# Seven block products in place of eight: the down-projections of a two-layer encoder

## The chip, the cores and the metric

The kernel runs on one core of one Trainium2 chip. The metric is the time of one execution in device microseconds (us). Five engines work side by side, each taking its own instructions in order: TensorE (PE, matmuls and weight loads), VectorE (DVE), ScalarE (ACT), GpSimd (POOL) and SyncE (SP, which issues the large transfers).

## The reference, cut to what matters

256 positions of width 2048 pass through two layers. Each has a token mixer (layer 0: grouped-query attention, layer 1: dilated window attention) and a gated MLP; every sub-layer is preceded by an RMS norm and added to the residual `h`, and a last norm follows.

```python
def conv_ffn(h, w_up, conv_w, conv_b, w_down):
    u = h @ w_up                       # 2048 -> 2 x 5632
    u = depthwise_conv3(u, conv_w) + conv_b
    gate, val = jnp.split(u, 2, axis=-1)
    return (jax.nn.silu(gate) * val) @ w_down   # 5632 -> 2048
```

All of it is float32. The change concerns the last product, `@ w_down`, in both layers.

## The kernel before, in words

**Precision.** Each operand of a large matmul is split into a high part of type F32R and the remainder, and each product is made of three: high x high, high x low, low x high (lines 115 to 117). The activations are the stationary operand, 128 tokens at a time; a weight tile is the moving operand with 512 columns.

**A feed** (`feed`, lines 97 to 135) is the unit of work. It takes 512 rows of a weight matrix (a chunk, `kg`) by 512 columns (a block, `n`): two transfers of 512 KB into `raw` buffers (line 105), of which there are four; for each, ACT makes the high part `wh` (line 127) and DVE the remainder `wl` (line 128), in four buffers each; then 2 x 2 x 2 x 3 matmuls into two PSUM banks, one per half of the tokens. A feed has 24 matmuls, 12 for each pair of `wh` and `wl`. The splits stand in `tc.high_priority(offset=AHEAD)`, so that the framework, which fixes each engine's order when the program is built, places them ahead of other work. `project` runs the feeds of a block one after another; `project2` interleaves two blocks such that the last chunk of both comes at the end; `project_last` handles the very last block so that its output can leave in pieces.

**The MLP** (`ffn`, lines 362 to 566) runs in two halves of 6 and 5 chunks of the hidden dimension (`HALVES`). For each chunk two up-projection blocks are computed (gate and value). What follows each block is written as generators (`gate_gen`, `value_gen`, `act_split`, `flush`), which `step()` advances a piece at a time between matmul groups: evacuation by ACT (line 359), 32x32 transposes by DVE and 16 copies by POOL (`turned`, lines 401 to 408), convolution taps on ACT and DVE (lines 388 and 396), the product of gate and value on POOL (line 422), and the split of the result (lines 441 and 442), which makes the stationary operands of the down-projection. A half then ends with four down-projection blocks of 512 columns over its 6 or 5 chunks (lines 557 to 564): `project2` for blocks 0 and 1, `project` for 2 and 3, in layer 1's second half `project_last` for block 3. `done` adds a block's two banks to `h` on DVE (line 331, or 487 at the end); in the second half of layer 0 it also starts the transposition of `h` for the next mixer (`late_transpose`, lines 273 to 307: transposes at line 268, splits at 213 and 216, copies at 263 and 297). In layer 1's second half POOL multiplies the finished blocks by the final gain (line 489).

PSUM has eight banks here: four `acc` tiles and four `ps` tiles. `bias_lines` (line 866) prepares the bias table of mixer B on the side.

Of the kernel before, what the change touches and what calls it, by code (L numbers as in the profile page):

```python
# [7 lines left out]
F32 = mybir.dt.float32  # L8
# [22 lines left out]
def tile_encoder(ctx: ExitStack, tc: tile.TileContext, x, xT, w_a, w_ao, q_gain, k_gain, w_b, w_bo,  # L31
# [17 lines left out]
    ones = cpool.tile([P, P], F32, name="ones")  # L49
    nc.gpsimd.memset(ones, 1.0)  # L50
# [46 lines left out]
    def feed(accs, lhs, kg, wap, first, last, by_m=False, pieces=1, mid=None):  # L97
# [11 lines left out]
        def mms(order):  # L109
            for m, kt in order:  # L110
                (wh, wl), j = hls[kt // 2], kt % 2
                xh, xl = lhs[4 * kg + kt][:2]
                st, sp = first and kt == 0, last and kt == 3
# [159 lines left out]
    def late_transpose(hT, n, g, pool, tag):  # L273
# [5 lines left out]
        if n < 3:  # L279
            t = pool.tile([P, 4, NT], F32, tag=tag, name=nm("tT"))  # L280
# [81 lines left out]
    def ffn(l, hT, ss_in, cw, g_next, last, side=None):  # L362
        with tc.tile_pool(name=nm("fpool"), bufs=1) as fp:
            junk = junk_of(fp)
            next_space[0] = fp, ("quad", 2), ("tT", 1)
# [5 lines left out]
            if last:  # L371
                fin = fp.tile([P, D], F32, name="fin")
                nc.gpsimd.dma_start(fin, final_norm.partition_broadcast(P))
# [27 lines left out]
            def turned(s, u):  # L401
# [3 lines left out]
                for q, c in QC:  # L405
                    nc.gpsimd.tensor_copy(u[32 * c:32 * c + 32, :, :, 32 * q:32 * q + 32],  # L406
                                          quad[32 * q:32 * q + 32, c].rearrange("p (j m) t -> p j m t", m=2))
# [16 lines left out]
            def value_gen(accs, blk, gate, last):  # L424
                s = evac_scaled(fp, accs, rstd, 1)
                yield
                turned(s, blk[1])
# [8 lines left out]
            def act_split(value):  # L436
                slots, k0 = value[5:]
                cv = value[2]
                for j in range(4):
# [3 lines left out]
                    if j == 1:  # L443
                        yield

# [11 lines left out]
            kgs = list(range(4))  # L457
            for hf, (p0, p1) in enumerate(HALVES):
                slots = {}
                last_value = None  # L460
                for p in range(p0, p1):
# [16 lines left out]
                    if p == 1 and side is not None:  # L478
                        spare.append(side())
                start(flush(last_value))  # L480

                def done(accs, n):
                    if hf == 1 and last:
                        for m in range(2):
# [4 lines left out]
                            nc.gpsimd.tensor_tensor(hs, hs, fin[:, cols], ALU.mult)  # L489
# [5 lines left out]
                    if hf == 1:  # L495
                        sumsq_cols(ss, n, junk)
                        start(late_transpose(hTn, n, g_next, fp, "tT"))
# [14 lines left out]
                def put(m, c0, c1, how, r):  # L512
                    hs = h[:, m, c0:c1]
                    if how == "fin":
                        nc.vector.scalar_tensor_tensor(hs, hs, r, fin[:, c0:c1], ALU.mult, ALU.mult)
# [19 lines left out]
                def last_out(acc, parts):  # L535
# [8 lines left out]
                    nc.gpsimd.tensor_tensor(ha, ha, fin[:, 1536:1536 + NT], ALU.mult)  # L544
# [628 lines left out]
```

## Time and profile before

| | |
|---|---|
| median of 3 timed runs | 2253.71 us (2253.49 to 2254.2) |
| profiled execution, first to last instruction | 2253.4 us |
| granted TensorE clock, mean | 0.999 |
| down-projection stages, layer 0 | 519 to 650 us and 867 to 977 us |
| down-projection stages, layer 1 | 1789 to 1919 us and 2136 to 2245 us |
| moved by DMA | 439.56 MB, 195 GB/s |

The profile is one execution, whose span is given from its first to its last instruction; no other time of it is recorded. Its page lists busy time by engine, the chain of work that ended last, and the costliest groups of instructions. The trace behind it answers questions about a stretch of time (windows), about the order of instructions (timeline) and about one line. A group's row reads: line, engine, operation, output and inputs with their shapes, count, then busy us and mean ns of one, then the idle time of that engine in front of them and what ended it. A row of one line reads: count, shortest, median and longest duration in ns.

### The profile page before, as it was taken

To read this page: it belongs to the slowest core of one execution; us is meant where nothing else is said; L and a number is where in the kernel's file an instruction comes from. 1 tells how busy PE (TensorE), PEld (TensorE's weight loads), DVE (VectorE), ACT (ScalarE), POOL (GpSimd) and SP (SyncE) were. 2 spreads that over 40 slices of the span, in tenths; PEclk is the share of its full clock that TensorE was granted. 3 is DMA by queue.
4 is the path that set the end of the run, shared out by engine and by line. 5 is a ranking of instruction groups with operands and counts; after the bars stand their busy time and mean duration, and the time that the engine had idled before them with its cause. 6 is when DMAs were issued, how large, how long until landed. Compare 5 with 4: busy or idle time off the path is not lost.

```text
span 2253.4 us, 28552 instructions
## 1 busy us (share of the span) xinstructions
PE 2240.8 (99%) x10089; PEld 1860.1 (83%) x10089; DVE 1605.8 (71%) x2137; ACT 1216.2 (54%) x1691; POOL 760.4 (34%) x999
## 2 busy tenths in 40 slices
PE   9999999999999999999999999999999999999998
PEld 7888888888888888888888888888888888888887
DVE  6877967776546777878876877676777764576765
ACT  7676556555345655555454554445655543465653
POOL 2342165663006554010052007002665600256530
PEclk9999999999999999999999999999999999999999
DMA  8565665655555565565566555566555555555554
GB/s 302 191 222 172 203 201 190 195 193 195 194 193 192 194 193 188 191 215 195 184 191 195 180 187 175 180 201 211 195 193 193 193 196 192 193 195 194 191 196 150
DMA packets 125871, 439.56 MB, mean 195 GB/s; under 512 B 14232, under 2 KB 18072, under 8 KB 125600
## 3 DMA queue, kind: packets, MB, share of 16 engines
q1 hardware_dynamic: 123056, 429.05, 57.0%
q0 software_dynamic: 2384, 8.39, 1.5%
q8 instruction: 79, 1.29, 0.2%
q14 instruction: 64, 0.52, 0.1%
q10 hardware_dynamic: 288, 0.30, 0.0%
HBM read 432.34 MB, written 5.34 MB: 194 GB/s over the span
## 4 chain that ended last, share of the span: by engine, by line
PE 96%; DVE 2%; DMA 1%; issue 1%; POOL 1%; ACT 0%; SPq 0%; DVEq 0%; POOLq 0%; ACTq 0%
PE acc L116 31%; PE acc L115 31%; PE acc L117 31%; DVE wl L128 1%; DMA raw<-in_w_b_dram 1%; DVE tT L268 1%; PE ps L225 0%; PE ps L224 0%; PE ps L223 0%; PE ps L1031 0%; PE ps L221 0%; DMA raw<-in_w_a_dram 0%; ACT wh L127 0%; POOL wide L263 0%; POOL t L704 0%
## 5 line engine op out<-in xcount | busy, mean ns | idle before, releaser
L128 DVE TENSOR_TENSOR wl<-raw,wh 128x1024 fp32r<-128x1024 f32 (+1 forms) x804 | 1010.0, 1260 | 521.2 <-ACT wh L127 518.1
L127 ACT ACTIVATE wh<-raw 128x1024 fp32r<-128x1024 f32 (+1 forms) x804 | 840.8, 1050 | 800.7 <-PE acc L117 714.8
L115 PE MATMUL acc<-wh,xh 128*128 128x512 f32 x2176 | 848.7, 390 | 0.7 <-ACT wh L127 0.7
L116 PE MATMUL acc<-wl,xh 128*128 128x512 f32 x2176 | 847.6, 390 | 0.3 <-DVE wl L128 0.2
L117 PE MATMUL acc<-wh,xh 128*128 128x512 f32 x2176 | 847.3, 389 | 0.0
L406 POOL COPY u<-quad 32x256 f32<-32x256 f32 x704 | 489.4, 695 | 539.9 <-DVE quad L259 512.1
L117 PEld LDWEIGHTS acc<-wh,xh 128*128 128x128 f32 x2176 | 408.6, 188 | 85.5
L115 PEld LDWEIGHTS acc<-wh,xh 128*128 128x128 f32 x2176 | 408.8, 188 | 84.8 <-ACT wh L127 1.1
L116 PEld LDWEIGHTS acc<-wl,xh 128*128 128x128 f32 x2176 | 408.8, 188 | 84.5 <-DVE wl L128 1.4
L115 PE MATMUL acc<-wh,a 128*128 128x512 f32 x1008 | 392.8, 390 | 0.0
L116 PE MATMUL acc<-wl,a 128*128 128x512 f32 x1008 | 392.3, 389 | 0.0
L117 PE MATMUL acc<-wh,a 128*128 128x512 f32 x1008 | 392.2, 389 | 0.0
L117 PEld LDWEIGHTS acc<-wh,a 128*128 128x128 f32 x1008 | 189.2, 188 | 39.5 <-DVE a L210 0.2
L116 PEld LDWEIGHTS acc<-wl,a 128*128 128x128 f32 x1008 | 189.3, 188 | 39.0
L115 PEld LDWEIGHTS acc<-wh,a 128*128 128x128 f32 x1008 | 189.3, 188 | 38.6
L263 POOL COPY wide<-quad 32x256 f32<-32x256 f32 x165 | 107.2, 650 | 170.1 <-DVE quad L259 162.9
L422 POOL TENSOR_TENSOR cv<-cg,cv 128x1024 f32<-128x1024 f32 x22 | 71.1, 3232 | 135.7 <-DVE cv L396 135.7
L359 ACT ACTIVATE stg<-acc,rstd 128x512 f32<-128x512 f32 x122 | 82.9, 685 | 31.7 <-PE acc L117 31.7
L396 DVE SCALAR_TENSOR_TENSOR cg<-u,cw,cg 128x256 f32<-128x256 f32 x176 | 82.3, 511 | 4.5 <-ACT cg L388 4.5
L396 DVE SCALAR_TENSOR_TENSOR cv<-u,cw,cv 128x256 f32<-128x256 f32 x176 | 74.3, 479 | 15.5 <-ACT cv L388 15.3
L259 DVE STREAM_TRANSPOSE quad<-stg 128x512 f32<-128x512 f32 x88 | 59.4, 699 | 10.3 <-ACT stg L359 10.3
L268 DVE STREAM_TRANSPOSE tT<-h 32x256 f32<-32x256 f32 x144 | 62.8, 436 | 2.7
(172 smaller groups left out, 1037.0 us busy)
## 6 DMA issues: line engine op xcount, KB each, us to landing
raw<-in_w_up_dram SPq DMA_DIRECT2D x352, 512.0 KB, 4.5
raw<-in_w_down_dram SPq DMA_DIRECT2D x176, 512.0 KB, 4.2
raw<-in_w_b_dram SPq DMA_DIRECT2D x144, 512.0 KB, 4.4
raw<-in_w_bo_dram SPq DMA_DIRECT2D x48, 512.0 KB, 3.7
raw<-in_w_a_dram SPq DMA_DIRECT2D x40, 512.0 KB, 4.7
raw<-in_w_ao_dram SPq DMA_DIRECT2D x32, 512.0 KB, 4.0
raw<-in_w_a_dram SPq DMA_DIRECT2D x16, 256.0 KB, 5.8
there<-quad POOLq DMA_DIRECT2D x6, 512.0 KB, 3.2
```

Of the source, the lines that this page charges most:

```text
L115: nc.tensor.matmul(accs[m], xh[:, c], wh[:, j, :], start=st, stop=False)
L116: nc.tensor.matmul(accs[m], xh[:, c], wl[:, j, :], start=False, stop=False)
L117: nc.tensor.matmul(accs[m], xl[:, c], wh[:, j, :], start=False, stop=sp)
L127: nc.scalar.activation(wh[:, c], r[:, c], AF.Copy)
L128: nc.vector.tensor_tensor(wl[:, c], r[:, c], wh[:, c].bitcast(F32), ALU.subtract)
L259: nc.vector.transpose(quad[:, :, at, :], src.rearrange("p (x c t) -> p c x t", c=4, t=32))
L263: nc.gpsimd.tensor_copy(o[32 * c:32 * c + 32, :, 32 * q:32 * q + 32], quad[32 * q:32 * q + 32, c])
L268: nc.vector.transpose(o[cols].rearrange("p a (m t) -> p a m t", m=2)[:, :, :, rows], s[rows].rearrange("p m (a c) -> p a m c", c=P)[:, :, ...
L359: nc.scalar.activation(o[:, m, :], accs[m], AF.Copy, scale=rstd[:, m:m + 1])
L396: nc.vector.scalar_tensor_tensor(cj, halves(flat[:, j, o:o + NT])[:, ::-1], tap(n, j, i), cj, ALU.mult, ALU.add)
L406: nc.gpsimd.tensor_copy(u[32 * c:32 * c + 32, :, :, 32 * q:32 * q + 32], quad[32 * q:32 * q + 32, c].rearrange("p (j m) t -> p j m t", m=2))
L422: made.append(nc.gpsimd.tensor_tensor(cv, cg, cv, ALU.mult).ins)
```

## The change

In each half of each MLP, two of the chunks (the first and the third, `fast = (0, 2)`) are multiplied for two column blocks at a time in seven products of half-size blocks, in Winograd's form of Strassen's scheme. The 512 rows of the chunk are cut into two halves of 256, the tokens into two halves of 128, and the two column blocks are the third pair. Eight products of such blocks would be 48 matmuls; the seven are 42.

- `combined` (called by `act_split`) builds the sums of activations for the two chunks: four subtractions on DVE and three larger splits.
- `fast_unit` loads the four weight quarters of the two blocks, forms four sums of 128x1024 (two on POOL, two on DVE, one of these in place), splits seven tiles, and issues 7 x 6 matmuls into the banks of products 1 to 7.
- `fold` adds products 1, 5, 6 and 7 into `h`: one copy on ACT, four additions on DVE that read PSUM, four on POOL. Products 2, 3 and 4 share the banks into which the ordinary feeds of the remaining chunks accumulate.
- `pair` runs two blocks over all chunks in a given order and takes all eight PSUM banks. The orders differ by half; in layer 1's second half the last two blocks run both fast units first, then `project` and `project_last` over the other chunks.
- Room is made: the final gain is loaded in four pieces just before layer 1's last down-projections, into buffers of `hT`; an unused constant goes; some temporaries share buffers; nine of the sixteen copies of the last value block of each half go from POOL to ACT.

```diff
+                if k0 // 4 in fast:
+                    slots[-1 - k0 // 4] = combined(cv, k0)
+                    ready.add(k0 // 4)
...
+            def combined(cv, k0):
+                v = cv.rearrange("p (b j) (m t) -> p b j m t", b=2, m=2)
+                st = fp.tile([P, 4, 2, P], F32, tag="sum", name=nm("st"), bufs=3)
+                a11, a21, a12, a22 = v[:, 0, :, 0], v[:, 0, :, 1], v[:, 1, :, 0], v[:, 1, :, 1]
+                for o, x, y in ((0, a21, a22), (2, a21, a11), (1, a11, st[:, 0]), (3, a12, st[:, 1])):
+                    nc.vector.tensor_tensor(st[:, o], x, y, ALU.subtract)
...
+                split_in_order(*own, st)
+                split_in_order(hA, lA, v[:, :, :, 0])
+                split_in_order(hB, lB, a22)
...
+            def fast_unit(acc, pick, wap0, wap1, begun, first, end):
...
+                b11, b12, b22, b21 = load(wap0, 0), load(wap1, 0), load(wap1, 1), load(wap0, 1)
+                with tc.high_priority(offset=2 * AHEAD):
+                    t1 = new_sum()
+                    nc.gpsimd.tensor_tensor(t1, b11, b12, ALU.add)
+                    nc.vector.tensor_tensor(b12, b12, b22, ALU.add)
+                    t2 = new_sum()
+                    nc.vector.tensor_tensor(t2, b11, b12, ALU.add)
+                    t4 = new_sum()
+                    nc.gpsimd.tensor_tensor(t4, t2, b21, ALU.add)
+                for i, (q, r) in enumerate(((1, b11), (2, b21), (5, t1), (3, b22), (7, b12), (6, t2), (4, t4))):
...
+                    with tc.high_priority(offset=AHEAD):
+                        nc.scalar.activation(wh, r, AF.Copy)
+                        nc.vector.tensor_tensor(wl, r, wh.bitcast(F32), ALU.subtract)
+                    xh, xl = pick[q]
+                    for j in range(2):
...
+                        nc.tensor.matmul(acc[q], xh[:, j], wh[:, j], start=st, stop=False)
+                        nc.tensor.matmul(acc[q], xh[:, j], wl[:, j], start=False, stop=False)
+                        nc.tensor.matmul(acc[q], xl[:, j], wh[:, j], start=False, stop=sp)
+                    begun.add(q)
+                    step(i % 2 == 0)
+
+            def fold(acc, n0, n1):
...
+                nc.scalar.activation(a, acc[1], AF.Copy)
+                tt(v, acc[6], a, ALU.subtract)
+                pool(hs(0, n0), hs(0, n0), a, ALU.add)
+                tt(w, acc[7], v, ALU.add)
+                tt(c, acc[5], v, ALU.add)
+                pool(hs(0, n1), hs(0, n1), c, ALU.add)
+                tt(v, acc[5], w, ALU.add)
+                pool(hs(1, n0), hs(1, n0), w, ALU.subtract)
+                pool(hs(1, n1), hs(1, n1), v, ALU.add)
...
-                done(project2(wd, 0, 1, slots, list(range(np_)), 1, lambda a: done(a, 0)), 1)
-                for n in (2, 3):
-                    if last and hf == 1 and n == 3:
-                        project_last(wd, n, slots, list(range(np_)), first_out, last_out)
+                for n0, n1 in ((0, 1), (2, 3)):
+                    if last and hf == 1 and n0 == 2:
...
+                        for kg in fast:
+                            fast_unit(acc, slots[-1 - kg], wd[n0, kg], wd[n1, kg], begun, kg == fast[0],
+                                      range(1, 8) if kg == fast[-1] else ())
+                        fold(acc, n0, n1)
...
+                        rest = [kg for kg in range(np_) if kg not in fast]
+                        done(project(wd, n0, slots, rest), n0)
+                        project_last(wd, n1, slots, rest, first_out, last_out)
                     else:
-                        done(project(wd, n, slots, list(range(np_))), n)
+                        rest = [kg for kg in range(np_) if kg not in fast]
+                        both = {kg: [(kg, 0), (kg, 1)] for kg in rest}
+                        f0, f1 = ([(kg, None)] for kg in fast)
+                        if n0 == 0:
+                            order = both[1] + f0 + both[3] + (both[4] if np_ > 5 else []) + f1 + both[np_ - 1]
+                        elif hf == 0:
+                            order = f0 + both[1] + f1 + both[3] + both[4] + both[5]
+                        else:
+                            order = [(1, 0)] + f0 + [(3, 0)] + f1 + [(4, 0), (1, 1), (3, 1), (4, 1)]
+                        pair(wd, (n0, n1), slots, order, done)
```

More of the change, by code (lines that the diff above doesn't have):

```diff
@@ L95, in drain, with feed @@
                 step()
-    def feed(accs, lhs, kg, wap, first, last, by_m=False, pieces=1, mid=None):
+    def feed(accs, lhs, kg, wap, first, last, by_m=False, pieces=1, mid=None, begun=()):
         raws, w = [], 2048 // pieces
@@ L112, in mms @@
                 xh, xl = lhs[4 * kg + kt][:2]
-                st, sp = first and kt == 0, last and kt == 3
+                st, sp = first and kt == 0 and m not in begun, last and kt == 3
                 c = slice(m * P, (m + 1) * P)
@@ L364, in ffn @@
             junk = junk_of(fp)
[L365 removed]
+            next_space[0] = fp, ("quad", 2), ("cv", 1)
             drain(1)
```

143 lines of the change are left out of this document (104 added, 39 removed).

## The prediction

> **What bounds the kernel now.** I read the page first: busy times, then the chain, then the costliest groups.
>
> ```profile
> PE 2240.8 (99%) x10089; PEld 1860.1 (83%) x10089; DVE 1605.8 (71%) x2137; ACT 1216.2 (54%) x1691; POOL 760.4 (34%) x999
> PE 96%; DVE 2%; DMA 1%; issue 1%; POOL 1%; ACT 0%; SPq 0%; DVEq 0%; POOLq 0%; ACTq 0%
> L127 ACT ACTIVATE wh<-raw 128x1024 fp32r<-128x1024 f32 (+1 forms) x804 | 840.8, 1050 | 800.7 <-PE acc L117 714.8
> L422 POOL TENSOR_TENSOR cv<-cg,cv 128x1024 f32<-128x1024 f32 x22 | 71.1, 3232 | 135.7 <-DVE cv L396 135.7
> ```
>
> TensorE (PE) is busy throughout and is 96% of the chain. ScalarE (ACT) waits 714.8 us before L127 for PE to give back a `wh` buffer: the splits run as far ahead as four buffers let them. So fewer matmuls shorten the kernel, as long as the other engines deliver. Whether they do is read from the stages that change, the eight pairs of down-projection blocks. The windows view has one row for each: layer 0 first half, layer 0 second half, then layer 1. The last row is an up-projection.
>
> ```profile
> core 0: us, PE busy (x) PEld busy (x) DVE busy (x) ACT busy (x) POOL busy (x), PEclk, DMA share, GB/s
> 519.40:584.40 65.00, 65.00 (x289) 53.83 (x288) 42.34 (x49) 31.11 (x39) 13.93 (x17) 1.00 0.57 195
> 584.40:649.70 65.30, 65.30 (x290) 54.09 (x289) 31.84 (x29) 25.47 (x24) 0.00 (x0) 1.00 0.56 193
> 867.00:922.00 55.00, 55.00 (x244) 45.58 (x243) 39.94 (x51) 28.77 (x39) 13.92 (x17) 1.00 0.59 194
> 922.30:976.60 54.30, 54.30 (x241) 45.00 (x240) 49.60 (x80) 28.15 (x41) 0.00 (x0) 1.00 0.55 188
> 1789.00:1854.00 65.00, 65.00 (x288) 53.85 (x287) 42.34 (x48) 30.78 (x38) 13.93 (x17) 1.00 0.57 195
> 1854.00:1919.00 65.00, 65.00 (x289) 53.83 (x288) 31.54 (x29) 25.46 (x24) 0.00 (x0) 1.00 0.57 193
> 2136.00:2190.00 54.00, 54.00 (x240) 44.70 (x240) 37.29 (x45) 29.05 (x40) 16.29 (x19) 1.00 0.59 194
> 2190.00:2244.00 54.00, 54.00 (x245) 44.93 (x243) 30.70 (x30) 22.20 (x27) 7.37 (x6) 1.00 0.44 143
> 246.00:519.00 273.00, 272.96 (x1204) 225.35 (x1203) 199.03 (x254) 158.87 (x207) 149.02 (x200) 1.00 0.61 198
> ```
>
> PE never stops, at the full clock (1.00). VectorE (DVE) is second: it leaves 23 and 33 us idle in the two pairs of a six-chunk half, but only 15 and 4.7 us in layer 0's five-chunk half (rows 3 and 4).
>
> The timeline shows one period of the feeding pipeline:
>
> ```profile
> 620.13 1.06 ACT L127 ACTIVATE wh<-raw 128x1024 fp32r<-128x1024 f32 x1 [1.66 <-PE acc L117]
> 621.22 1.23 DVE L128 TENSOR_TENSOR wl<-raw,wh 128x1024 fp32r<-128x1024 f32 x1 [1.50 <-ACT wh L127]
> 622.85 1.06 ACT L127 ACTIVATE wh<-raw 128x1024 fp32r<-128x1024 f32 x1 [1.66 <-PE acc L117]
> ```
>
> The period is 2.72 us for 12 matmuls, so **0.2267 us a matmul**. A buffer is refilled 2.3 us after PE frees it (620.13 to 622.45) and needed after three further buffers, 8.2 us: the **lead is 5.8 us**.
>
> **What the change removes.** A pair's two blocks at one chunk take 48 matmuls; the seven products take 7 x 2 x 3 = 42. There are 2 fast chunks x 2 pairs x 2 halves x 2 layers = 16 units, so 96 matmuls go: 96 x 0.2267 = **21.8 us**, 2.72 per pair. The tail after the last matmul stays. The Trainium skill (TensorE: Matmul & The Clock Gate, Part 1) gives 215.7 ns from start to start for such a matmul; by it the gain would be 20.7 us. The trace has 227, and the trace decides.
>
> **What it adds on DVE and POOL.** A unit splits seven tiles instead of four and adds two sums on DVE: five more 128x1024 instructions with two SBUF inputs. It also puts two 128x1024 sums on GpSimd (POOL). Each pair gets a fold: four DVE instructions that read PSUM, and four 128x512 additions on POOL. Their prices, from the timeline of DVE and of POOL and the row of L772:
>
> ```profile
> L331 DVE TENSOR_TENSOR h<-acc,h 128x512 f32<-128x512 f32 x5 | 3.2, 681 | 0.0
> 967.99 3.49 DVE L128 TENSOR_TENSOR wl<-raw,wh 128x1024 fp32r<-128x1024 f32 x3
> 976.43 1.28 DVE L331 TENSOR_TENSOR h<-acc,h 128x512 f32<-128x512 f32 x2
> 538.04 4.55 DVE L128 TENSOR_TENSOR wl<-raw,wh 128x1024 fp32r<-128x1024 f32 x2
> 538.30 3.22 POOL L422 TENSOR_TENSOR cv<-cg,cv 128x1024 f32<-128x1024 f32 x1 [5.81 <-DVE cv L396]
> 2187.64 2.97 POOL L489 TENSOR_TENSOR h<-h,fin 128x512 f32<-128x512 f32 x2 [28.68 <-ACT junk L488]
> 2189.70 1.99 DVE L128 TENSOR_TENSOR wl<-raw,wh 128x1024 fp32r<-128x1024 f32 x1 [1.49 <-ACT wh L127]
> 409.33 3.23 POOL L422 TENSOR_TENSOR cv<-cg,cv 128x1024 f32<-128x1024 f32 x1 [6.44 <-DVE cv L396]
> 410.73 1.39 DVE L259 STREAM_TRANSPOSE quad<-stg 128x512 f32<-128x512 f32 x2 [0.44 <-ACT stg L359]
> L772 POOL TENSOR_TENSOR pr<-pr,l x14: 1032/1042/1940, 90.8 to 183.4; 128x512 f32<-128x512 f32 x14
> ```
>
> Three splits in a row take 3.49: the last shows its full 1.23, so one more occupies (3.49 - 1.23) / 2 = **1.13 us**. Two residual additions take 1.28, with one at 0.68 (row of L331): 0.60 for one more. At 538 two splits, worth 2.36, take 4.55, while L422 runs on POOL: DVE stood **2.19 us** for one POOL addition of the size that each unit gets twice. It happens again at 2189.70 with a 128x512 one. A POOL addition of 128x512 takes 1.04 undisturbed, which I take as its hold. Two transposes inside L422's next run (410.73) take 1.39, an ordinary pace: they are not held. An addition that reads PSUM, with one operand in SBUF, I count as not held either.
>
> The Trainium skill (SBUF — State Buffer, "Who interferes with whom") has the rule: a DVE instruction with two SBUF inputs and a GpSimd instruction that reads SBUF exclude each other, and the later one waits for the whole of the other. The trace agrees (4.55 for 2.36). By the Trainium skill, a DVE instruction with one SBUF input is free of it, and here too the trace agrees (the transposes at 410.73).
>
> So on DVE a unit occupies 9 x 1.13 + 2 x 2.19 = **14.6 us, against 9.5 us of PE** (42 x 0.2267). Per pair: 10 x 1.13 + 4 x 0.60 = 13.7 us of DVE work, and 4 x 2.19 + 4 x 1.04 = 12.9 us of holds.
>
> - Six-chunk halves: PE 288 x 0.2267 - 2.7 = 62.6 each. First pair 42.3 + 13.7 = 56.0, with holds 68.9; second 45.5, with holds 58.4. Sum 127.3 against 125.2.
> - Layer 0's five-chunk half: PE 240 x 0.2267 - 2.7 = 51.7 each. First pair 53.6, with holds 66.5; second 63.3, with holds 76.2. Sum 142.7 against 103.4: **39 us too much**, 13.5 of it without any hold.
> - Layer 1's: 51.0 and 44.4, with holds 63.9 and 57.3. Sum 121.2 against 103.4: **18 us too much**.
>
> **What is forgiven.** The lead of 5.8 us once per half. Holds that fall on instructions with one SBUF input: those that read PSUM, and transposes. Layer 0's second half has many transposes:
>
> ```profile
> L268 DVE STREAM_TRANSPOSE tT<-h 32x256 f32<-32x256 f32 x42 | 18.3, 436 | 0.8
> L216 DVE SCALAR_TENSOR_TENSOR xh<-tT,gain,xh 128x256 fp32r<-128x256 f32 x12 | 5.1, 478 | 0.6 <-ACT xh L213 0.6
> 542.52 0.75 DVE L442 TENSOR_TENSOR a<-cv,a 128x256 fp32r<-128x256 f32 x2
> L297 ACT ACTIVATE wide<-quad x18: 412/414/417, 264.3 to 1533.8; 32x256 f32<-32x256 f32 x18
> raw<-in_w_down_dram SPq DMA_DIRECT2D x176, 512.0 KB, 4.2
> ```
>
> With 18.3 us of transposes beside 26 us of holds I let half (13) overlap; some 5 us of transposes and their splits can slide into mixer B. Stalls of PE: layer 0 second half 39 - 13 - 5.8 - 5 = 15 (bounds 3 without holds' cost, 28 without overlap). Layer 1 second half: 18 - 5.8 - 3 (PSUM readers) = 9, and 6 more because its last pair runs both units back to back: 29.2 us of DVE against 19.0 of PE, the slack coming too late. That is 15 (bounds 3 and 24). A six-chunk half: the excess of its first pair, 68.9 - 62.6 = 6.3, is just what the lead and the PSUM readers cover; I take 1.5 each for the units that start a pair (bounds 0 and 6.3). Sum 15 + 15 + 3 = **33 us of stalls**, between 6 and 65.
>
> Edits at nothing: `combined` replaces four splits of 128x256 by four subtractions and three larger splits, some 2 us more DVE per fast chunk (four subtractions at 0.38, half of the row of L442, and an estimated 0.6 for 1792 columns of splits in place of 1024), in up-projections where DVE idles 74 of 273 us (last row of windows). Nine of the last value block's copies go from POOL to ACT, 9 x 0.41 = 3.7 us (row of L297), where ACT idles 24 to 34 us in these pairs; the lead covers them, and without it they cost that much once per half. The smaller loads of `fin`, the shared buffers and `bias_lines` stand off every path that PE waits on. The transfers are the same 2 MB per chunk; a unit holds all four `raw` buffers until its sums are done, which is priced under the second rival. A pair now holds all eight PSUM banks; the next pair's third product starts 2 x 1.36 us or more after its first, and the two residual additions in front of it (1.28) fit unless DVE is already behind, which is counted.
>
> Sum: the profiled execution's 2253.4 us of span lies 0.3 below the median of the timed runs, 2253.7; so 2253.7 - 21.8 + 33 = **2265 us**, slower by 0.5%.
>
> **Rivals.** *Holds cost nothing (faster).* POOL's sums fall into time in which DVE waits anyway, or under transposes and PSUM readers. For it: DVE alone exceeds PE only in layer 0's second half, 116.9 against 103.4; minus lead and slide (10.8) 3 us of stalls remain, and 3 for the back-to-back units: 2253.7 - 21.8 + 6 = 2238. It decides from where the holds that cost fall below 21.8 - 6 = 16 us of the 103 added. Against it: row 4 has 4.7 us of idle DVE for 13 of holds. When the sums are issued early enough the six-chunk halves give their full 10.9 in either case.
>
> *DVE's excess is paid in each unit (much slower).* A unit holds the four `raw` buffers until its sums and splits are done; if DVE is late, the next feed's loads start late, and each needs 4.2 us to land (row above), 1.06 and 1.23 for its split, 6.5 in all of the unit's 9.5. Then no lead builds up again between units: 16 x (14.6 - 9.5) = 82 us, 2253.7 - 21.8 + 82 = 2314. For it: the last unit of each layer's second half has one feed or none in front of it. Against it: the other fourteen follow two feeds or more, and two feeds with a unit are 4 x 1.13 + 14.6 = 19.1 us of DVE in 20.4 of PE. Half of that price is 2273, inside the forecast.
>
> *It takes out no matmuls* is excluded by the loop counts.
>
> **Numbers.** Forecast 0.52 (its own range 2251 to 2281: stalls midway between 33 and each bound), first rival 0.36 (2232 to 2249), second rival 0.12 (2281 to 2314). From 2237 to 2292 about 0.10 is left out below and 0.08 above. This kernel's measurement tells about 0.2% (4.5 us) from no change: below 2249.2 lies the first rival, 0.36; between, 0.10; above 2258.2, 0.54.
>
> **What would show it.** Right: 96 fewer matmuls; PE busy falling below its windows' length in the second halves, with waits of PE for `wl`; DVE over 95% there; splits of 3 us and more beside POOL's additions in the units; the six-chunk halves some 8 to 11 us shorter than now over both layers. Wrong: PE still full in all eight windows (then the first rival, 2238), or PE waiting for `raw` transfers in the six-chunk halves too (then the second). If the splits beside POOL's sums stay at 1.23 us, the step on holds has failed.

## The result, and the profile after

The changed kernel takes **2321.18 us** (median of 4 runs, 2319.83 to 2322.79) against 2253.95 (2253.49 to 2255.61) beside it: a ratio of 1.0295 (95% interval 1.028 to 1.0309), slower by 67 us. The sign of the forecast was right, its size was not: 2321 lies above the range.

The page of the kernel after, its busy times, its chain and two groups (lines in this section are those of the kernel after):

```profile
PE 2255.0 (97%) x9993; PEld 1851.8 (80%) x9993; DVE 1792.0 (77%) x2276; ACT 1286.7 (55%) x1775; POOL 909.4 (39%) x1029
PE 76%; DVE 13%; DMA 4%; POOL 3%; issue 3%; ACT 1%; SPq 0%; POOLq 0%; DVEq 0%; ACTq 0%
L490 POOL TENSOR_TENSOR sum<-raw,raw 128x1024 f32<-128x1024 f32 x16 | 43.0, 2686 | 155.3 <-DMA raw<-in_w_down_dram 155.3
L501 DVE TENSOR_TENSOR wl<-raw,wh 128x1024 fp32r<-128x1024 f32 x64 | 94.0, 1483 | 3.9 <-ACT wh L500 3.8
```

The 96 matmuls are gone (10089 to 9993), yet PE is busy 14 us longer. Of the 36 us between that and 22 us less, the halved clock (below) makes some 18; the rest isn't settled (the kernel without any sum, below, has 17 us more than the missing matmuls leave, with hardly any halved clock). PE's share of the chain fell from 96 to 76%; DVE has 13% and the transfers 4%. DVE is busy 186 us longer; POOL's first sum takes 2.69 us on average, and a split of a raw tile in the units 1.48 where one alone takes 1.23.

The windows of the kernel after, one for each pair of blocks, columns and order as in the view of before:

```profile
521.20:586.00 64.80, 62.77 (x269) 51.30 (x268) 58.34 (x58) 40.36 (x54) 26.47 (x16) 0.97 0.53 180
586.00:658.90 72.90, 67.62 (x286) 54.08 (x285) 57.01 (x48) 33.22 (x33) 20.36 (x9) 0.98 0.56 186
876.50:939.00 62.50, 55.78 (x230) 44.44 (x229) 57.79 (x58) 38.43 (x55) 28.16 (x17) 0.95 0.50 164
939.00:1008.10 69.10, 59.66 (x230) 44.38 (x228) 66.30 (x88) 33.35 (x43) 14.59 (x8) 0.93 0.41 143
1827.20:1892.00 64.80, 62.87 (x268) 51.00 (x267) 55.59 (x58) 39.65 (x54) 25.83 (x15) 0.97 0.53 180
1892.00:1965.50 73.50, 68.01 (x288) 54.28 (x287) 57.52 (x48) 33.90 (x33) 21.07 (x10) 0.98 0.56 184
2183.10:2239.00 55.90, 50.60 (x205) 40.28 (x204) 52.75 (x53) 34.95 (x49) 21.50 (x13) 0.94 0.49 165
2239.00:2311.00 72.00, 60.55 (x256) 47.11 (x255) 59.64 (x52) 32.00 (x40) 36.20 (x18) 0.98 0.37 125
```

PE is below its window in all eight rows, also in the six-chunk halves (rows 1, 2, 5, 6), where DVE has 6 to 16 us to spare in each row. So PE waits although DVE isn't full. From the first matmul of a stage to the first of the next, the time stands as follows (in the last line up to the end; mixer B up to its output projection; "full" is before less the saved matmuls at 0.2267 us):

| stage | before | full | after | lost |
|---|---|---|---|---|
| six chunks, layer 0 | 130.6 | 125.2 | 137.7 | 12.5 |
| five chunks, layer 0 | 108.8 | 103.4 | 131.6 | 28.2 |
| mixer B | 416.8 | 416.8 | 422.9 | 6.1 |
| six chunks, layer 1 | 130.6 | 125.2 | 138.3 | 13.1 |
| five chunks, layer 1, with the tail | 116.6 | 111.2 | 136.7 | 25.5 |

Together 85 us are lost; 22 are saved; some 3 more lie in other stages. Which waits they are, from the waits of the kernel after (in all, times, longest):

```profile
ACT wh L500 <- DMA raw<-in_w_down_dram: 44.5, 15, 4.9
PEld ps L507 <- DVE wl L501: 28.6, 21, 2.7
DVE raw L491 <- POOL sum L490: 22.1, 9, 3.1
PEld acc L507 <- DVE wl L501: 19.1, 15, 4.4
PE acc L506 <- DVE h L329: 6.0, 2, 3.2
PE acc L506 <- DVE h L601: 3.2, 1, 3.2
```

PE waits for the low parts of the units' tiles. ACT, ahead of that, waits for raw weights: 39.3 of the 44.5 us stand in front of the second tile of a unit, `b21`, which product 2 needs and which `fast_unit` loads last of the four quarters. DVE's sum in place (L491) waits until POOL (L490) has read the buffer that it overwrites. And three times, 9.2 us in all, the first unit of a second pair waits for a bank: its second product takes one that DVE has still to add to `h` (L329, L601), and this addition stands in DVE's queue behind the unit's sums and a split that POOL holds up.

The sixteen units take 9.6 to 18.8 us each, counted from the start of the first matmul to one step (0.23 us) behind the start of the last; 42 matmuls at 0.2267 make 9.5. The two with four feeds in front of them, both in six-chunk halves, take 9.6 and 10.0; the fourteen with three or fewer take 12.2 and more. Together they take 71 us too long, the halved clock included. The timeline of one unit, the second of layer 0's second half, which starts at 910.56, shows how the waits follow one another:

```profile
906.55 2.39 POOL L490 TENSOR_TENSOR sum<-raw,raw 128x1024 f32<-128x1024 f32 x1 [15.39 <-DMA raw<-in_w_down_dram]
908.90 2.40 POOL L431 TENSOR_TENSOR cv<-cg,cv 128x1024 f32<-128x1024 f32 x1
908.97 3.40 DVE L491 TENSOR_TENSOR raw<-raw,raw 128x1024 f32<-128x1024 f32 x1 [2.33 <-POOL sum L490]
911.33 0.42 ACT L455 ACTIVATE a<-cv 128x256 fp32r<-128x256 f32 x1 [6.71 <-POOL cv L431]
911.65 1.04 ACT L500 ACTIVATE wh<-raw 128x1024 fp32r<-128x1024 f32 x1
912.41 1.23 DVE L493 TENSOR_TENSOR sum<-raw,raw 128x1024 f32<-128x1024 f32 x1
912.74 0.50 PE L506 MATMUL acc<-wh,sx 128*128 128x512 f32 x1 [0.63 <-ACT wh L500]
913.77 2.41 POOL L495 TENSOR_TENSOR sum<-sum,raw 128x1024 f32<-128x1024 f32 x1 [2.48 <-DVE sum L493]
913.89 3.37 DVE L501 TENSOR_TENSOR wl<-raw,wh 128x1024 fp32r<-128x1024 f32 x1
917.31 0.80 PE L507 MATMUL acc<-wl,sx 128*128 128x512 f32 x1 [4.07 <-DVE wl L501]
918.33 0.63 PE L506 MATMUL acc<-wh,sx 128*128 128x512 f32 x1
918.76 0.63 PE L507 MATMUL acc<-wl,sx 128*128 128x512 f32 x1
```

Read it from the stall backwards. PE stands 4.07 us before 917.31 for a split that began at 913.89 and took 3.37, since L495 on POOL had begun at 913.77. That split, which product 2 needs, stood in DVE's queue behind both sums. The first of these waited 2.33 us for L490 and then took 3.40 beside L431. One wait and two holds make 2.3 + 2.3 + 2.1 us, all in front of the end of one split. They don't all count, though. The split couldn't have begun before 912.7, when ACT ended the high part (911.65). That in turn stood in ACT's queue behind a split of activations (L455), which had waited 6.71 us for POOL's product of gate and value (L431), itself behind L490. So from 912.7 on DVE's queue costs 1.2 us and the hold 2.1. After the stall the matmuls start 0.43 us apart (918.33, 918.76) instead of 0.227.

### The profile page after: what moved, and what is told of

It reads as the page before. It is cut to its first block, busy times and chain, and to the rows that moved or that the text cites. A ratio compares the mean times of both kernels' runs of the same rounds, so it can differ in the third digit from the quotient of the medians.

```text
span 2319.8 us, 28737 instructions
## 1 busy us (share of the span) xinstructions
PE 2255.0 (97%) x9993; PEld 1851.8 (80%) x9993; DVE 1792.0 (77%) x2276; ACT 1286.7 (55%) x1775; POOL 909.4 (39%) x1029
## 4 chain that ended last, share of the span: by engine, by line
PE 76%; DVE 13%; DMA 4%; POOL 3%; issue 3%; ACT 1%; SPq 0%; POOLq 0%; DVEq 0%; ACTq 0%
PE acc L114 24%; PE acc L115 24%; PE acc L113 24%; DVE wl L501 5%; DMA raw<-in_w_down_dram 3%; DVE wl L126 3%; POOL u L414 2%; POOL sum L490 1%; DVE tT L266 1%; DVE raw L491 1%; DVE sum L493 1%; DVE a L456 1%; ACT wh L125 0%; PE ps L223 0%; DMA raw<-in_w_b_dram 0%
## 5 line engine op out<-in xcount | busy, mean ns | idle before, releaser
L126 DVE TENSOR_TENSOR wl<-raw,wh 128x1024 fp32r<-128x1024 f32 (+1 forms) x740 | 934.0, 1270 | 356.7 <-ACT wh L125 353.4
L125 ACT ACTIVATE wh<-raw 128x1024 fp32r<-128x1024 f32 (+1 forms) x740 | 774.7, 1049 | 682.9 <-PE acc L115 567.3
L114 PE MATMUL acc<-wl,a 128*128 128x512 f32 x752 | 293.9, 391 | 3.9 <-DVE wl L126 3.9
L113 PE MATMUL acc<-wh,a 128*128 128x512 f32 x752 | 293.5, 391 | 0.0
L115 PE MATMUL acc<-wh,a 128*128 128x512 f32 x752 | 293.1, 390 | 0.0
L114 PEld LDWEIGHTS acc<-wl,a 128*128 128x128 f32 x752 | 141.6, 188 | 34.5 <-DVE wl L126 5.7
L115 PEld LDWEIGHTS acc<-wh,a 128*128 128x128 f32 x752 | 141.5, 188 | 29.7 <-DVE a L208 0.2
L113 PEld LDWEIGHTS acc<-wh,a 128*128 128x128 f32 x752 | 141.4, 188 | 29.3 <-ACT wh L125 0.2
L431 POOL TENSOR_TENSOR cv<-cg,cv 128x1024 f32<-128x1024 f32 x22 | 68.6, 3117 | 136.6 <-DVE cv L401 125.5
L500 ACT ACTIVATE wh<-raw 128x1024 fp32r<-128x1024 f32 x64 | 67.2, 1055 | 66.7 <-DMA raw<-in_w_down_dram 44.5
L490 POOL TENSOR_TENSOR sum<-raw,raw 128x1024 f32<-128x1024 f32 x16 | 43.0, 2686 | 155.3 <-DMA raw<-in_w_down_dram 155.3
L501 DVE TENSOR_TENSOR wl<-raw,wh 128x1024 fp32r<-128x1024 f32 x64 | 94.0, 1483 | 3.9 <-ACT wh L500 3.8
```

Of the source, the lines that this page charges most:

```text
L113: nc.tensor.matmul(accs[m], xh[:, c], wh[:, j, :], start=st, stop=False)
L114: nc.tensor.matmul(accs[m], xh[:, c], wl[:, j, :], start=False, stop=False)
L115: nc.tensor.matmul(accs[m], xl[:, c], wh[:, j, :], start=False, stop=sp)
L125: nc.scalar.activation(wh[:, c], r[:, c], AF.Copy)
L126: nc.vector.tensor_tensor(wl[:, c], r[:, c], wh[:, c].bitcast(F32), ALU.subtract)
L431: made.append(nc.gpsimd.tensor_tensor(cv, cg, cv, ALU.mult).ins)
```

## The experiments

Theory 1 puts the loss down to POOL's two sums in a unit (the holds, and what waits for them). Theory 2 is the second rival: the unit as such, with DVE's work and the `raw` buffers that it keeps. Single runs of before on these chips took 2254.4 to 2256.7, so each result is also given against the run of before beside it; a difference of under 2 us between two single runs tells nothing. Where a line of a kernel is quoted, its number is that of that kernel.

**No products at all, the other edits kept.**

```diff
-            fast, ready = (0, 2), set()
+            fast, ready = (), set()
```

> No chunk is multiplied in seven products; the blocks run as before the change, and every other edit stays (smaller loads of the final gain, shared buffers, nine copies on ACT). All theories that put the loss into the fast units expect 2254 us within 4. If the other edits carry a part of the 67 us, it shows here.

2255.74, 1.3 above before (2254.44). The copies on ACT, the pieces of `fin` and the shared buffers cost nothing that shows; the loss belongs to the units.

**POOL's two sums onto DVE.**

```diff
-                    nc.gpsimd.tensor_tensor(t1, b11, b12, ALU.add)
+                    nc.vector.tensor_tensor(t1, b11, b12, ALU.add)
...
-                    nc.gpsimd.tensor_tensor(t4, t2, b21, ALU.add)
+                    nc.vector.tensor_tensor(t4, t2, b21, ALU.add)
```

> The two sums that POOL made are made by DVE; the same result. Theory 1 (DVE stands for POOL: holds of the shared port, and the in-place sum that must wait for POOL's reading): the 88 us of stalls fall to about 25, so 2257 us, though DVE has 32 instructions of 1.13 us more. Theory 2 (DVE has simply too much work of its own): 36 us of DVE more, so 2321 to 2355. Theory 3 (the four raw buffers are given back late, so loads are late): 2310 to 2325.

2310.66, 56.2 above before. Only 11 us came back: theory 1 alone falls. Two sums cost about two thirds as much as work on DVE as they do on POOL (by the next run 21 and 32 us).

**POOL's two sums left out.**

```diff
-                    nc.gpsimd.tensor_tensor(t1, b11, b12, ALU.add)
...
-                    nc.gpsimd.tensor_tensor(t4, t2, b21, ALU.add)
-                for i, (q, r) in enumerate(((1, b11), (2, b21), (5, t1), (3, b22), (7, b12), (6, t2), (4, t4))):
+                for i, (q, r) in enumerate(((1, b11), (2, b21), (5, b11), (3, b22), (7, b12), (6, t2), (4, b21))):
```

> The two sums on POOL are left out: products 5 and 4 use unsummed quarters, so the values of the down-projections change and the time shows the unit without POOL's part. Theory 1: stalls near 10 us, 2240 to 2250. Theory 2: DVE's work is unchanged, 2300 to 2321. Theory 3: the raw buffers come back a little earlier, 2300 to 2315.

2289.61, 35.2 above before, 32 below the changed kernel. So POOL's sums cost 32 us, under half of what is lost.

**The sum of `b12` and `b22` into a buffer of its own**, so that DVE needn't wait for POOL's reading; `t4` goes over `b12`.

```diff
-                    nc.vector.tensor_tensor(b12, b12, b22, ALU.add)
+                    t3 = new_sum()
+                    nc.vector.tensor_tensor(t3, b12, b22, ALU.add)
...
-                    t4 = new_sum()
+                    t4 = b12
```

> The sum of b12 and b22 goes into a buffer of its own instead of over b12, so DVE need not wait until POOL has read b12; the last sum of POOL goes over b12 instead. Theory 1, if the wait in the queue is its larger part (DVE waits 22 us for POOL in front of this sum, and splits stand behind it): 2285 to 2300. Theory 1, if the holds are its larger part: 2312 to 2325. Theories 2 and 3: 2315 to 2325.

2327.28, 72.8 above before: slower than the change. DVE's wait for POOL (22.1 us) is gone from its waits, but PE waits longer for the splits:

```profile
PEld acc L508 <- DVE wl L502: 32.2, 20, 3.2
PEld ps L508 <- DVE wl L502: 31.2, 20, 3.2
```

So taking this wait away doesn't pay by itself. What it is worth alone the run doesn't show: with `t4` over `b12` a `raw` buffer is held up to the last split of the unit, and ACT's waits for these transfers rise from 59 us (44.5 in the units, 14.1 in the feeds) to 95 (57.2 and 37.8). That may be why it is 5.6 us slower than the change; no run parts the two.

**The products in the six-chunk halves alone.**

```diff
+                fast = (0, 2) if hf == 0 else ()
```

> Only the six-chunk halves use the seven products; the five-chunk halves run as before. If each half's loss is its own, the changed kernel's stages say +7.1 and +7.7 us for these two, so 2266 to 2272. If part of their loss spills into what follows, more. The prediction's step (six-chunk halves gain 8 to 11 us) would give 2243 to 2246.

2279.14, 24.2 above before. The six-chunk halves take 140.6 and 140.5 us against 130.6 before. There, where the forecast saw 127.3 us of DVE for 125.2 of PE, the units lose as surely as elsewhere.

**The products with raw weights first**, the sums in the queue behind their splits.

```diff
-                with tc.high_priority(offset=2 * AHEAD):
...
-                for i, (q, r) in enumerate(((1, b11), (2, b21), (5, t1), (3, b22), (7, b12), (6, t2), (4, t4))):
+                for i, (q, r) in enumerate(((1, b11), (2, b21), (3, b22), (5, t1), (7, b12), (6, t2), (4, t4))):
+                    if i == 3:
+                        with tc.high_priority(offset=AHEAD):
+                            sums()
```

> In a unit the three products whose weights need no sum go first, and the sums are placed behind their splits with the splits' own priority; the same result. Theory A (order: splits that are due stand on DVE behind sums that are due later): the waits in products 2 and 3, about 50 of the 88 us, mostly go, 2275 to 2295. Theory B (DVE and the holds together have more work than the stage has time, whatever the order): 2310 to 2325.

2313.27, 58.4 above before: the order is worth 8 to 9 us.

**The same order with all four sums on DVE.**

```diff
-                    nc.gpsimd.tensor_tensor(t1, b11, b12, ALU.add)
+                    nc.vector.tensor_tensor(t1, b11, b12, ALU.add)
...
-                    nc.gpsimd.tensor_tensor(t4, t2, b21, ALU.add)
+                    nc.vector.tensor_tensor(t4, t2, b21, ALU.add)
```

> The same order, with all four sums on DVE. Theory A: 2260 to 2280. Theory B: as with the sums on DVE alone, 2305 to 2315.

2301.11, 46.2 above before: 21 us better than the change, and still far from gain.

**No sums at all**, seven splits kept.

```diff
-                    nc.gpsimd.tensor_tensor(t1, b11, b12, ALU.add)
-                    nc.vector.tensor_tensor(b12, b12, b22, ALU.add)
-                    nc.vector.tensor_tensor(t2, b11, b12, ALU.add)
-                    nc.gpsimd.tensor_tensor(t4, t2, b21, ALU.add)
-                for i, (q, r) in enumerate(((1, b11), (2, b21), (5, t1), (3, b22), (7, b12), (6, t2), (4, t4))):
+                for i, (q, r) in enumerate(((1, b11), (2, b21), (5, b11), (3, b22), (7, b12), (6, b12), (4, b21))):
```

> All four weight sums are left out (the products use plain quarters, so the values change); seven splits per unit and the folds remain. Theory A: no sum stands before a split, 2235 to 2250. Theory B: per pair 13.7 - 4.5 = 9.2 us of DVE and 4.2 of holds remain, an excess in layer 0's second half alone (116.9 + 8.4 - 9 = 116 against 103): 2242 to 2256. Above 2260: the seven splits themselves, each feeding only 1.36 us of PE, are too close for the lead.

2272.17, 17.3 above before. Without any sum the units still lose 39 us, against 22 saved; the sums make up some 50 of the 89 that the change loses.

**The last kernel with two POOL additions that nobody reads**, for the hold by itself.

```diff
+                    nc.gpsimd.tensor_tensor(new_sum(), b11, b12, ALU.add)
+                    nc.gpsimd.tensor_tensor(new_sum(), b22, b21, ALU.add)
```

> As without any sum, but POOL makes two additions of 128x1024 per unit whose results nobody reads; DVE makes none and waits for none. Only the hold of the shared port is left of POOL's part. Theory B (holds count as DVE work): 70 us of holds at the rate at which DVE's own two sums cost (17 us for 36) are some 30, so 2295 to 2310. If POOL's part costs through the waits for its results, 2272 to 2280.

2306.59, 49.9 above before: 33 us more than without them, though nobody waits for their results. The page of the kernel without sums, then of this one:

```profile
PE 2236.5 (99%) x9993; PEld 1839.2 (81%) x9993; DVE 1702.2 (75%) x2244; ACT 1281.3 (56%) x1775; POOL 813.9 (36%) x997
L493 DVE TENSOR_TENSOR wl<-raw,wh 128x1024 fp32r<-128x1024 f32 x112 | 145.1, 1334 | 48.4 <-ACT wh L492 48.0
```

```profile
PE 2248.9 (98%) x9993; PEld 1844.9 (80%) x9993; DVE 1746.7 (76%) x2244; ACT 1284.9 (56%) x1775; POOL 898.4 (39%) x1029
L496 DVE TENSOR_TENSOR wl<-raw,wh 128x1024 fp32r<-128x1024 f32 x112 | 170.3, 1559 | 38.1 <-ACT wh L495 37.6
```

DVE issues the same 2244 instructions and is busy 44.5 us longer. One split of it in the timeline, beside the addition on POOL that holds it:

```profile
560.73 2.72 POOL L489 TENSOR_TENSOR sum<-raw,raw 128x1024 f32<-128x1024 f32 x1 [4.25 <-DMA raw<-in_w_down_dram]
561.11 3.42 DVE L496 TENSOR_TENSOR wl<-raw,wh 128x1024 fp32r<-128x1024 f32 x1
```

So holds exist and cost: 44.5 us of the 70 that 32 additions of 2.19 would make, and the kernel takes 33 us longer. Some 7 of the 33 are matmuls at half the clock. Another explanation would be that POOL's reading keeps the `raw` buffers longer; but ACT's waits for these transfers stay as they were, 111 us without the additions and 107 with them.

**No sums, and three of the four quarters in buffers of their own**, so that the unit leaves the `raw` buffers to the feeds.

```diff
-                b11, b12, b22, b21 = load(wap0, 0), load(wap1, 0), load(wap1, 1), load(wap0, 1)
+                b11, b21, b12, b22 = load(wap0, 0), load(wap0, 1, True), load(wap1, 0, True), load(wap1, 1, True)
```

> As without any sum, but three of a unit's four weight quarters are loaded into the unused sum buffers, so the four raw buffers are left to the feeds. Theory C (late raw buffers are what is left of the stalls once the sums are gone): 2240 to 2258. Theory B (DVE's seven splits and the folds): 2266 to 2274.

2254.86, 1.8 below before and 19 below the kernel without sums. From that one it differs in two things: the buffers, and the order of the loads, in which `b21` (for product 2) now comes second instead of last. The waits for transfers of the kernel with shared buffers, then of this one:

```profile
ACT wh L125 <- DMA raw<-in_w_down_dram: 64.5, 56, 3.0
ACT wh L492 <- DMA raw<-in_w_down_dram: 46.3, 16, 7.3
```

```profile
ACT wh L125 <- DMA raw<-in_w_down_dram: 21.7, 10, 5.6
ACT wh L492 <- DMA raw<-in_w_down_dram: 20.0, 6, 4.0
```

The windows of the whole six-chunk and five-chunk half of layer 0 with own buffers:

```profile
520.00:645.70 125.70, 125.70 (x554) 103.61 (x554) 91.03 (x97) 73.40 (x86) 21.41 (x16) 1.00 0.58 189
863.30:976.30 113.00, 108.90 (x457) 86.63 (x456) 100.02 (x138) 71.20 (x98) 20.37 (x16) 0.97 0.51 164
```

The six-chunk half runs with PE full. ACT's waits for transfers fall from 111 us to 42, and 19 us of time go. The feeds' part (L125, from 64.5 to 21.7) speaks for theory 2's second part, buffers kept too long. The units' part (L492, from 46.3 to 20.0) speaks for the order: in front of a unit's second tile 43 us become 0.8. How the 19 us divide between the two isn't shown. The kernel with four splits, below, shows that a late `b21` needn't cost anything where it is needed one product later: 42 us of such waits stand there, and PE is all but full.

**All sums on DVE and in place, behind the raw splits, two quarters in own buffers**: what the last runs pointed to, with the sums done.

```diff
-                b11, b12, b22, b21 = load(wap0, 0), load(wap1, 0), load(wap1, 1), load(wap0, 1)
+                b11, b21, b12, b22 = load(wap0, 0), load(wap0, 1), load(wap1, 0, True), load(wap1, 1, True)
...
+                    nc.vector.tensor_tensor(b11, b11, b12, ALU.add)
+                    nc.vector.tensor_tensor(b21, b11, b21, ALU.add)
```

> All four sums on DVE, behind the first three splits, and made in place, so that two quarters can be loaded into buffers of the unit's own; the same result. Theory C: 2270 to 2288, against 2301 with the raw buffers shared. Theory B: 2296 to 2304.

2308.45, 51.8 above before: a miss, 5.6 us worse than the same order of products with `raw` buffers. Matmuls at half the clock make 13 us in it and 12 in the other, so that is hardly the difference. In place, the sums keep two `raw` buffers up to the unit's last splits, and the feeds' waits for transfers rise from 20.5 us to 46.1; whether that alone undid what the other buffers should have brought stays open.

**One fast chunk for each pair**, built like the last, after two feeds or more.

```diff
-            fast, ready = (0, 2), set()
+            fast, ready = (0,), set()
...
+                            order = both[1] + both[2] + f0 + sum((both[kg] for kg in rest[2:]), [])
```

> One fast chunk instead of two, its unit behind two or more feeds, with the buffers and the order of the run before; the same result. 48 matmuls go, 10.9 us. If a unit behind two feeds costs no stall, as the first units of the halves show in the last runs, 2244 to 2250. If each us of DVE work and hold added (some 115) costs 0.4 to 0.5 us wherever it stands, 2285 to 2300.

2278.64, 22.0 above before. But the two units in the second pairs of the six-chunk halves, behind four feeds of their pair, took 9.6 us, the full pace; the other six took 11.7 to 14.9. Five of these had two feeds of their pair in front. The sixth, in layer 0's second half, had four like the two that were free, but stood beside the transposes for the next mixer on DVE, and it was the slowest. Whether the feeds in front or the quieter place (no activations made beside them) makes the two free, the last run below tells.

**No sums and only four splits**, each used by the products that share it.

```diff
+                    if id(r) not in done_:
...
+                        done_[id(r)] = wh, wl
+                    wh, wl = done_[id(r)]
```

> No sums, and only four splits per unit (one per weight quarter, each used by one or two products, so the values change); 42 matmuls per unit as in the changed kernel. DVE's work per pair is that of the kernel before plus the fold (2.4 us, and 4.2 of holds). Theory B (DVE work and holds are all of the loss): 2233 to 2246. If units cost through something else (all four quarters needed within the first products, eight banks), 2255 or more.

2240.48, 15.3 below before. The windows of layer 0's two halves, and the page:

```profile
520.50:646.10 125.60, 125.60 (x553) 103.57 (x552) 80.38 (x85) 61.63 (x74) 22.29 (x16) 1.00 0.64 201
863.70:968.50 104.80, 104.19 (x458) 85.52 (x456) 92.06 (x131) 58.76 (x86) 22.25 (x16) 1.00 0.60 193
PE 2223.2 (99%) x9993; PEld 1840.4 (82%) x9993; DVE 1648.7 (74%) x2196; ACT 1237.1 (55%) x1727; POOL 819.4 (37%) x997
```

With DVE at 92 of 104.8 us PE is all but full. This is the saving that the matmuls bring when little else is in their way. The three further splits cost 33 us, together with what goes with them: `raw` buffers held longer, and `b21` needed by the second product instead of the third.

**The same without the fold.**

```diff
-                tt(v, acc[6], a, ALU.subtract)
...
-                pool(hs(1, n1), hs(1, n1), v, ALU.add)
```

> As the run before, and the fold is left out too: four copies of 8 columns on ACT stand for it, so products 1, 5, 6 and 7 do not reach the output. Theory B: the full gain of the missing matmuls, 2230 to 2237. If above 2242, something in the units beside DVE and POOL costs.

2239.61, 16.1 below before: the fold costs 1 us, and less than single runs tell apart.

**One fast chunk in the six-chunk halves alone, behind four to six feeds**, sums on DVE in place, own buffers: four units, 24 matmuls fewer.

```diff
+                fast = (0,) if hf == 0 else ()
...
+                            order = both[1] + both[2] + both[3] + [(0, None)] + both[4] + both[5]
+                        else:
+                            order = both[1] + both[2] + [(0, None)] + both[3] + both[4] + both[5]
```

> Seven products for one chunk in the six-chunk halves alone, behind four to six ordinary feeds, with all sums on DVE in place; the same result as the kernel before. 4 units take out 24 matmuls, 5.4 us; two more activations sums in the up-projections cost about 1. If units in the slack of these halves are free, 2248 to 2252; if they still cost half of their DVE work, 2258 to 2266.

2251.72 (median of 11 runs, 2250.5 to 2252.34) against 2255.75 (15 runs, 2254.53 to 2256.98): a ratio of 0.9981 (95% interval 0.9972 to 0.999), faster by 4.0 us where 24 x 0.2267 makes 5.4. The 1.4 us between lie in the up-projections, where the sums of activations are made. All four units run at 9.6 us, those in a first pair too, which stand behind six feeds, with the last splits of activations between their own. The window of its first six-chunk half:

```profile
520.10:648.20 128.10, 128.10 (x566) 105.89 (x565) 97.82 (x99) 67.67 (x80) 22.36 (x16) 1.00 0.61 189
```

PE is full, with DVE at 97.8 of 128.1 us. This version beats both kernels, by little.

## Why the prediction was right or wrong

The runs, put in order, build the loss up step by step. Time is against the run of before beside each; DVE is its busy time on the page.

| step | against before | step | DVE's rise |
|---|---|---|---|
| 96 matmuls at 0.2267 | -21.8 | | |
| units without sums and fold, four splits | -16.1 | +5.7 | 12.9 |
| fold | -15.3 | +0.8 | 30.0 |
| three more splits on ACT and DVE, `b21` needed earlier | +17.3 | +32.6 | 53.5 |
| two sums on DVE | +35.2 | +17.9 | 43.5 |
| two sums on POOL (the change) | +67.2 | +32.0 | 46.3 |

- **Gain, 21.8: right.** The count is exact, and with four splits and no sums 15.3 of it is seen. Of the 5.7 that are missing without the fold, 1.3 lie in the up-projections: `combined`, which was priced at nothing. The other edits of that paragraph cost nothing that shows, with one exception, the banks (below).
- **Holds: right in kind.** In the two kernels shown splits of 3.37 and 3.42 us stand beside POOL's additions, as the prediction asked. The full sum of 70 us for the units' additions was too much, 44.5 of it occurred.
- **The fold, with 4 x 1.04 us of holds a pair and 4 x 0.60 of work: too dear.** Where no sums stand beside it, it adds 30 us to DVE's busy time and about 1 us to the kernel's.
- **What is forgiven: the step that failed.** The prediction set the sum of DVE's work against PE's time for a whole half, and took off a lead of 5.8 us, half of the holds, and a slide into mixer B. It came to 33 us of stalls. The stages lost 85: 12.5 and 13.1 where the six-chunk halves were given 1.5 each (upper bound 6.3), 34 with mixer B's start where layer 0's second half was given 15 (upper bound 28), 25.5 where layer 1's was given 15 (upper bound 24). All four lie above the bounds. It wasn't that DVE had more to do than forecast. With all holds in it, it was busy 115 us in a six-chunk half (rows 1 and 2 of the windows after, 58.3 and 57.0), where the forecast had 127.3 and PE's work alone is 125.2; 124 in layer 0's second half for 142.7; 112 in layer 1's for 121.2. So no total of DVE's work could have shown the loss. Two of its signs failed with it: the six-chunk halves, to be 8 to 11 us shorter over both layers, are 15 longer; and DVE "over 95%" is 94% in layer 0's second half (57.8 and 66.3 of 131.6 us), 88% in layer 1's (52.8 and 59.6 of 127.9).
- **What took its place** is the second rival's mechanism: the excess is paid in each unit. A unit needs all four quarters by its fourth product, and the one loaded last by its second; its sums stand in the queue ahead of splits that are due earlier; and it keeps the `raw` buffers, so that the next feeds come late and no lead builds up. Three runs show parts of it: own buffers and `b21` loaded second take away 19 us, the order of the sums 8 to 9, and in the six-chunk halves four to six feeds in front of a unit all of its stalls. The rival's price, 2314, came nearest; its chance of 0.12 was too low. That it came so near is partly luck: it charges every unit 5.1 us, with holds of 70 us of which some 45 occurred and without the clock, where the units lost 0 to 9 us, 71 in all, and the rest stands between them. Its "against" (two feeds and a unit are 19.1 us of DVE in 20.4 of PE) was the same error: it compares sums where the order decides.
- **A term at nothing: the banks.** The prediction has the next pair's third product take a bank of the pair before, 2 x 1.36 us after its first. It is the second product, 1.36 us after, and the residual additions stand behind the unit's sums on DVE. PE waited 9.2 us for them, in three places.
- **A term that was missing: the clock.** The trace of before shows 1.00 in every stage, and the forecast priced a stall at its own length. In the kernel after, 90 matmuls in and between the changed stages have the next one 0.43 us behind them; at 0.2 each more than the usual that is up to **18 us** of the 85. Up to, since a slower PE also gives DVE time to catch up; no run shows the stages with the clock kept up.

What stays open: whether buffers held longer are all of why the sum in its own buffer and the sums in own buffers were each some 6 us slower than their counterparts, and how the 32.6 us of the three splits divide between work, buffers held longer and the late `b21`. The change with nothing but `b21` loaded second wasn't run. Apart from the change itself and the last version, each kernel was timed once.

## What to carry to other kernels

A saving of matmuls on a bound TensorE is worth what the feeding engines can deliver within each block of work, not over the stage: list for each tile when it must land, which queue it stands in, and when its buffer comes free. The order of a unit's loads belongs on that list. Added work on an engine that is busy 75% of the time cost very different amounts here, though idle time was there on the page: 30 us of fold cost about 1 us of the kernel's time, while sums and splits in front of a waiting product cost 0.4 to 0.7 us for each us. Such a scheme pays where units are rare and stand behind enough ordinary work, and nothing else presses on the feeding engine: four of them gave 4 us, sixteen took 67.

## What the runs showed of the hardware

Behind stalls of PE the clock fell. The windows of the kernel after around the stall shown above:

```profile
905.00:912.50 7.50, 7.12 (x32) 5.52 (x30) 5.13 (x5) 1.18 (x2) 4.74 (x2) 1.00 0.28 105
912.50:916.50 4.00, 0.50 (x1) 0.19 (x1) 4.00 (x3) 4.00 (x8) 2.41 (x1) 0.97 0.35 113
916.50:923.20 6.70, 5.89 (x14) 4.64 (x15) 6.70 (x8) 2.23 (x3) 1.39 (x1) 0.51 0.33 108
923.20:927.00 3.80, 3.80 (x19) 3.10 (x18) 3.41 (x4) 2.53 (x4) 0.00 (x0) 1.00 0.69 236
```

The granted clock is 0.51 for 6.7 us, in which 14 matmuls start instead of some 29, and then 1.00 again. The kernel after has eleven such stretches within the changed stages and just behind them, nine of 3.41 us and two of 6.83. They begin 2.5 to 3.9 us after the start of a gap of 2.3 to 4.6 us between two matmuls, or (once) behind two of 1.2 and 1.4; gaps of 3.6 us at 2245.6 and of 2.4 at 890.2 were followed by none.

What decides shows in the starts of these stretches, which stand multiples of 3.413 us apart. Cut into windows on this raster from 500 us on, the traces of the kernel after and of the fifteen kernels of the experiments show the same: a window at full clock in which at most 5 matmuls started (15 fit) was followed by the half clock every time (48 of 48), one with 6 or 7 in 13 of 65 cases, one with 8 or more never. So a gap counts by how much of it falls into one window, and two short ones in a window do as well.

The Trainium skill (TensorE: Matmul & The Clock Gate, Part 1) has the clock fall to half after an idle window of about 3.4 us, with matmuls of 512 columns then 426.7 ns apart. The trace agrees on the pace (0.43 us) and on a window of that length; as to the trigger, the window needn't be idle throughout: gaps of 2.3 and 2.4 us sufficed here.

Unexpected as well: a buffer that POOL still reads stops an in-place sum on DVE for 2.3 us, and everything behind it in the queue, which the dependence alone does not show as a cost until the order of the queue is read.
